# Where the low halves of the down weights come from: a subtraction on VectorE, or an accumulating transfer from GpSimd's queue

## The chip, the core and the metric

One core of a Trainium2 chip runs the whole program. The metric is device time in microseconds (us), the median of the runs taken. The engines are named as the profile names them: PE is TensorE (its matmuls), PEld its weight loads, DVE is VectorE, ACT is ScalarE, POOL is GpSimd, and SP the engine whose queue issues the loads.

## The reference

One layer over 256 tokens with a model width of 2048. What matters here are the two SwiGLU blocks, one near the start and one near the end, with 5632 hidden columns:

```python
def _swiglu(x, wg, wu, wd):
    return (jax.nn.silu(x @ wg) * (x @ wu)) @ wd

h = h + 0.5 * _swiglu(_rmsnorm(h, ffn1_norm[i]), ffn1_wg[i], ffn1_wu[i], ffn1_wd[i])
...
h = h + 0.5 * _swiglu(_rmsnorm(h, ffn2_norm[i]), ffn2_wg[i], ffn2_wu[i], ffn2_wd[i])
```

Between them stand an attention and short-convolution mixer with its own projections, and behind the second a gated embedding and a final norm. All weights are float32.

## The kernel before

Every weight matrix is streamed once from HBM in blocks of 512 rows by 512 columns. Such a block is a tile `raw` of 128 partitions by 2048 float32 values (1 MB); four `raw` buffers exist, and SP issues each load as soon as a buffer is free (`fetch`, line 84).

The products are made in three passes so as to keep float32 accuracy. Each operand is split into a high half `hi`, which is the value rounded to the float32r type that PE multiplies, and a low half `lo`, which is the rest. For every product `mm3` (line 100) issues three matmuls into the same PSUM bank: high by high (L101), high activations by low weights (L102), low activations by high weights (L103).

The weights are split on the way, half a `raw` tile (128 x 1024) at a time, by `split` (line 89): ACT copies the half into `whi`, which rounds it, and DVE subtracts `whi` from `raw` into `wlo`. There are five `whi` and five `wlo` buffers. One such half is here called a **step**; it feeds 12 matmuls: two blocks of 128 rows, two blocks of 128 tokens, three passes. Each step's first matmul (L101) waits for its `whi`, the next (L102) for its `wlo`.

`unit` (line 111) makes one output block of 512 columns: it loops over the `raw` tiles, over their two halves, and issues the matmuls. `pump` runs small queued pieces of work (transposes and splits of activations) between steps.

`swiglu` (line 230) goes through the 11 hidden blocks in three parts of 4, 4 and 3. In each part come the gate and up products of these blocks and the split of the gated result, and then the part's **down stage**: four `unit` calls with the name `ffn1d` or `ffn2d`, one for each 512 columns of the output, over the 4, 4 or 3 blocks just made. A down stage has 32, 32 or 24 steps, so there are 88 steps in each SwiGLU block and 176 in six stages overall. After each `unit` DVE adds half the result to `h` (line 266); in the third part the squares for the next norm follow on ACT.

The order within each engine is that of the program as written, with small moves by the scheduler; every engine works through its own queue in order, and a waiting instruction holds up what stands behind it.

Of the kernel before, what the change touches and what calls it, by code (L numbers as in the profile page):

```python
# [14 lines left out]
ALU = mybir.AluOpType  # L15
# [18 lines left out]
def block_kernel(ctx, tc, x, xT, pT, cols, fin, bias, mask,  # L34
                 wg1, wu1, wd1, win, wout, wg2, wu2, wd2, wpg, wpp, out):
    nc = tc.nc
# [6 lines left out]
    def act(out, in_, func=AF.Copy, **kw):  # L43
        nc.scalar.activation(out=out, in_=in_, func=func, **kw)  # L44
# [4 lines left out]
    def f(ap):  # L49
        return ap.bitcast(F32)  # L50
# [24 lines left out]
    def big(j, name):  # L75
        return (work.tile([P, 4, SEQ], F32R, tag=f"gh{j}", name=name + "h", bufs=1),
                work.tile([P, 4, SEQ], F32R, tag=f"gl{j}", name=name + "l", bufs=1))

    def wk(name):
        return work.tile([P, 512], F32, tag="wk", name=name, bufs=WK)  # L80
# [3 lines left out]
    def fetch(src, name):  # L84
        raw = wpool.tile([P, 2048], F32, tag="raw", name=f"raw_{name}", bufs=4)
        nc.sync.dma_start(out=raw, in_=src)
        return raw

    def split(raw, o, name, parts=1):
        hi = wpool.tile([P, 1024], F32R, tag="whi", name=f"whi_{name}", bufs=5)  # L90
        lo = wpool.tile([P, 1024], F32R, tag="wlo", name=f"wlo_{name}", bufs=5)
        n = 1024 // parts
        for i in range(parts):
            sl = slice(i * n, (i + 1) * n)
            rsl = slice(o + i * n, o + (i + 1) * n)
            act(hi[:, sl], raw[:, rsl])
            tt(out=lo[:, sl], in0=raw[:, rsl], in1=f(hi[:, sl]), op=ALU.subtract)  # L97
        return hi, lo

    def mm3(ps, xh, xl, wh, wl, first, last):  # L100
        nc.tensor.matmul(ps, lhsT=xh, rhs=wh, start=first, stop=False)  # L101
        nc.tensor.matmul(ps, lhsT=xh, rhs=wl, start=False, stop=False)  # L102
        nc.tensor.matmul(ps, lhsT=xl, rhs=wh, start=False, stop=last)  # L103
# [3 lines left out]
    def pump(n=1):  # L107
        for _ in range(min(n, len(queue))):
            queue.popleft()()

    def unit(w, n, name, lhs, flush_at=None, starting=False, hook=None):
        ps = [psum.tile([P, 512], F32, tag="mm", name=f"{name}_{t}") for t in range(2)]
        ng = 4 if flush_at is not None else len(lhs)
        for g in range(ng):
            if g == flush_at:
                pump(len(queue))
            if starting:
                raw = wpool.tile([P, 2048], F32, tag="raw", name=f"raw_{name}_{g}", bufs=4)
                m = 1 if g == 0 else 2
                for i in range(0, 4, m):  # L120
                    load_xT(g, i, m)
                    isl = slice(i * 512, (i + m) * 512)
                    nc.sync.dma_start(out=raw[:, isl], in_=w[n, g][:, isl])
            else:
                raw = fetch(w[n, g], f"{name}_{g}")
                if hook is not None:
                    hook(g)
            xh, xl = lhs[g]
            for s in range(2):
                hi, lo = split(raw, s * 1024, f"{name}_{g}_{s}", 2 if starting else 1)  # L130
                for j in range(2):
                    k = s * 2 + j
                    kk = g * 4 + k
                    for t in range(2):
                        tsl = slice(t * P, (t + 1) * P)
                        mm3(ps[t], xh[:, k, tsl], xl[:, k, tsl],
                            hi[:, j * 512:(j + 1) * 512], lo[:, j * 512:(j + 1) * 512],
                            kk == 0, kk == ng * 4 - 1)
                pump()
        return ps  # L140
# [20 lines left out]
    def rstd_of(which, only=None):  # L161
        nm = f"{which}_{only}"
        tsel = (0, 1) if only is None else (only,)
        n = len(tsel)
        s = small.tile([P, n], F32, tag="sm", name=f"sm_{nm}")
        for i, t in enumerate(tsel):
            nc.vector.tensor_reduce(out=s[:, i:i + 1], in_=stats[which, t][:, 0:nslot[which, t]],
                                    op=ALU.add, axis=AX.X)
        s2 = small.tile([P, n], F32, tag="sm2", name=f"sm2_{nm}")
        nc.vector.tensor_scalar(out=s2, in0=s, scalar1=1.0 / D, scalar2=EPS,  # L170
                                op0=ALU.mult, op1=ALU.add)
        r = small.tile([P, n], F32, tag="rstd", name=f"rstd_{nm}", bufs=4)
        nc.gpsimd.tensor_tensor(out=r, in0=s2, in1=mhalf[:, 0:n], op=ALU.pow)
        return r
# [15 lines left out]
    def finish_chunk(which, c):  # L190
        for p in range(2):
            queue.append(partial(next_aT, which, c, p))
        for t in range(2):
            square_stat(which, c, t)
# [3 lines left out]
    def load_xT(c, k0, n):  # L198
        if c not in xraw:
            xraw[c] = work.tile([P, 4, SEQ], F32, tag="y", name=f"xT_{c}", bufs=2)  # L200
        raw = xraw[c]
        nc.sync.dma_start(out=raw[:, k0:k0 + n, :],
                          in_=xT[c].rearrange("p (k s) -> p k s", k=4)[:, k0:k0 + n, :])
        for k in range(k0, k0 + n):
            g = col[:, c * 4 + k:c * 4 + k + 1]
            act(aTh[c][:, k, :], raw[:, k, :], scale=g)
            stt(out=aTl[c][:, k, :], in0=raw[:, k, :], scalar=g, in1=f(aTh[c][:, k, :]),
                op0=ALU.mult, op1=ALU.subtract)
# [21 lines left out]
    def swiglu(nm, nxt, wg, wu, wd, first):  # L230
        rstd = None
        chunk = 0
        for third, cnt in enumerate((4, 4, 3)):
            gs = []
            for j in range(cnt):
                fc = chunk + j
                pg = unit(wg, fc, f"{nm}g{fc}", aT, starting=first and fc == 0)
                if first and fc == 0:
                    pu = unit(wu, fc, f"{nm}u{fc}", aT, hook=load_x)
                if rstd is None:  # L240
                    rstd = rstd_of(nm)
                sg = []
                for t in range(2):
                    s = wk(f"{nm}sg{fc}_{t}")
                    act(s, pg[t], AF.Silu, scale=rstd[:, t:t + 1])
                    sg.append(s)
                if not (first and fc == 0):
                    pu = unit(wu, fc, f"{nm}u{fc}", aT)
                gt = []
                for t in range(2):  # L250
                    g = wk(f"{nm}gt{fc}_{t}")
                    stt(out=g, in0=pu[t], scalar=rstd[:, t:t + 1], in1=sg[t],
                        op0=ALU.mult, op1=ALU.mult)
                    gt.append(g)
                dst = big(j, f"{nm}g{fc}")
                for p in range(2):
                    queue.append(partial(pair_major, gt, p, f"{nm}gT{fc}", dst))
                gs.append(dst)
            last = third == 2
            wdt = wd[:, chunk:chunk + cnt]  # L260
            chunk += cnt
            for c in range(4):
                po = unit(wdt, c, f"{nm}d{third}_{c}", gs)
                for t in range(2):
                    hs = h[t][:, c * 512:(c + 1) * 512]
                    stt(out=hs, in0=po[t], scalar=0.5, in1=hs, op0=ALU.mult, op1=ALU.add)
                if last:
                    finish_chunk(nxt, c)

    swiglu("ffn1", "mix", wg1, wu1, wd1, True)  # L270

    rstd = rstd_of("mix")
# [181 lines left out]
    for c in range(4):  # L454
        po = unit(wout, c, f"o{c}", mixed, flush_at=3 if c == 0 else 4)
# [3 lines left out]
        finish_chunk("ffn2", c)  # L459

    swiglu("ffn2", "ple", wg2, wu2, wd2, False)

    rstd = rstd_of("ple")
# [24 lines left out]
    for c in range(4):  # L488
        if c % 2 == 0:
            raw = fetch(wpp[c // 2], f"pp{c}")  # L490
        hi, lo = split(raw, (c % 2) * 1024, f"pp{c}")
# [22 lines left out]
    for g in range(4):  # L514
        raw = fetch(wpg[3, g], f"pg3_{g}")
        xh, xl = aT[g]
        for s in range(2):
            hi, lo = split(raw, s * 1024, f"pg3_{g}_{s}")
# [110 lines left out]
```

## Time and profile before

| | us |
|---|---|
| median of 2 runs (1965.91 to 1966.38) | 1966.14 |
| span of the profiled execution | 1964.3 |
| PE busy in it | 1951.8 (99%) |
| DVE busy | 1039.3 (53%) |
| ACT busy | 902.6 (46%) |
| POOL busy | 35.2 (2%) |

The span runs from the first to the last instruction of the one profiled execution. It lies 1.8 us below the median of the runs, so a change worked out on the span is carried over to the median by adding 1.8 us.

### The profile page before, as it was taken

To read this page: it belongs to the slowest core of one execution; us is meant where nothing else is said; L and a number is where in the kernel's file an instruction comes from. 1 tells how busy PE (TensorE), PEld (TensorE's weight loads), DVE (VectorE), ACT (ScalarE), POOL (GpSimd) and SP (SyncE) were. 2 spreads that over 40 slices of the span, in tenths; PEclk is the share of its full clock that TensorE was granted. 3 is DMA by queue.
4 is the path that set the end of the run, shared out by engine and by line. 5 is a ranking of instruction groups with operands and counts; after the bars stand their busy time and mean duration, and the time that the engine had idled before them with its cause. 6 is when DMAs were issued, how large, how long until landed. Compare 5 with 4: busy or idle time off the path is not lost.

```text
span 1964.3 us, 21885 instructions
## 1 busy us (share of the span) xinstructions
PE 1951.8 (99%) x8889; PEld 1615.7 (82%) x8889; DVE 1039.3 (53%) x1064; ACT 902.6 (46%) x1121; POOL 35.2 (2%) x36
## 2 busy tenths in 40 slices
PE   9999999999999999999999999999999999999998
PEld 7888888888888888888888888888888888888886
DVE  5545554455545465665655554454445554445664
ACT  7444334444344454555545544443444433444554
POOL 0000000000000000110000000000000000000011
PEclk9999999999999999999999999999999999999999
DMA  9555555555555555544555555555555555555552
GB/s 353 199 190 192 193 193 193 190 186 187 194 193 187 193 179 185 193 172 161 182 184 186 180 190 193 190 186 195 195 185 188 190 193 193 193 192 184 201 182 105
DMA packets 55541, 374.01 MB, mean 190 GB/s; under 512 B 6416, under 2 KB 6928, under 8 KB 11408
## 3 DMA queue, kind: packets, MB, share of 16 engines
q1 hardware_dynamic: 55440, 372.62, 52.9%
q8 instruction: 69, 1.13, 0.2%
q14 instruction: 32, 0.26, 0.0%
HBM read 370.50 MB, written 2.10 MB: 190 GB/s over the span
## 4 chain that ended last, share of the span: by engine, by line
PE 99%; DMA 0%; issue 0%; SPq 0%; ACT 0%; DVE 0%; ACTq 0%; POOLq 0%; POOL 0%
PE ffn2g L101 4%; PE ffn2d L101 4%; PE ffn2g L103 4%; PE ffn1d L103 4%; PE ffn1d L101 4%; PE ffn2d L103 4%; PE ffn2g L102 4%; PE ffn2u L101 4%; PE ffn1u L101 4%; PE ffn1u L102 4%; PE ffn2d L102 4%; PE ffn2u L103 4%; PE ffn1u L103 4%; PE ffn2u L102 4%; PE ffn1d L102 4%; PE ffn1g L101 4%
## 5 line engine op out<-in xcount | busy, mean ns | idle before, releaser
L97 DVE TENSOR_TENSOR wlo_ffn2u<-raw_ffn2u,whi_ffn2u 128x1024 fp32r<-128x1024 f32 x88 | 107.8, 1226 | 131.6 <-ACT whi_ffn2u L44 131.6
L97 DVE TENSOR_TENSOR wlo_ffn1u<-raw_ffn1u,whi_ffn1u 128x1024 fp32r<-128x1024 f32 x88 | 107.5, 1226 | 124.0 <-ACT whi_ffn1u L44 124.0
L97 DVE TENSOR_TENSOR wlo_ffn2g<-raw_ffn2g,whi_ffn2g 128x1024 fp32r<-128x1024 f32 x88 | 107.9, 1226 | 112.9 <-ACT whi_ffn2g L44 112.9
L97 DVE TENSOR_TENSOR wlo_ffn1d<-raw_ffn1d,whi_ffn1d 128x1024 fp32r<-128x1024 f32 x88 | 107.9, 1226 | 112.2 <-ACT whi_ffn1d L44 112.2
L97 DVE TENSOR_TENSOR wlo_ffn2d<-raw_ffn2d,whi_ffn2d 128x1024 fp32r<-128x1024 f32 x88 | 107.9, 1226 | 111.4 <-ACT whi_ffn2d L44 111.4
L97 DVE TENSOR_TENSOR wlo_ffn1g<-raw_ffn1g,whi_ffn1g 128x1024 fp32r<-128x1024 f32 (+1 forms) x96 | 108.2, 1136 | 101.7 <-ACT whi_ffn1g L44 101.7
L44 ACT ACTIVATE whi_ffn2g<-raw_ffn2g 128x1024 fp32r<-128x1024 f32 x88 | 93.4, 1061 | 141.2 <-PE ffn2u L103 66.4
L44 ACT ACTIVATE whi_ffn1g<-raw_ffn1g 128x1024 fp32r<-128x1024 f32 (+1 forms) x96 | 94.2, 988 | 133.7 <-PE ffn1u L103 63.0
L44 ACT ACTIVATE whi_ffn1d<-raw_ffn1d 128x1024 fp32r<-128x1024 f32 x88 | 93.4, 1061 | 135.2 <-PE ffn1d L103 110.3
L44 ACT ACTIVATE whi_ffn2d<-raw_ffn2d 128x1024 fp32r<-128x1024 f32 x88 | 93.4, 1061 | 133.8 <-PE ffn2d L103 108.9
L44 ACT ACTIVATE whi_ffn2u<-raw_ffn2u 128x1024 fp32r<-128x1024 f32 x88 | 93.2, 1060 | 120.3 <-PE ffn2g L103 73.1
L44 ACT ACTIVATE whi_ffn1u<-raw_ffn1u 128x1024 fp32r<-128x1024 f32 x88 | 92.8, 1059 | 113.6 <-PE ffn1g L103 66.4
L101 PE MATMUL ffn1g<-whi_ffn1g,aTh 128*128 128x512 f32 x352 | 138.1, 395 | 1.5 <-ACT whi_ffn1g L44 1.5
L101 PE MATMUL ffn2g<-whi_ffn2g,aTh 128*128 128x512 f32 x352 | 138.8, 394 | 0.0
L102 PE MATMUL ffn1g<-wlo_ffn1g,aTh 128*128 128x512 f32 x352 | 137.3, 390 | 0.0
L103 PE MATMUL ffn1g<-whi_ffn1g,aTl 128*128 128x512 f32 x352 | 137.2, 390 | 0.0
L103 PE MATMUL ffn2g<-whi_ffn2g,aTl 128*128 128x512 f32 x352 | 137.2, 390 | 0.0
L102 PE MATMUL ffn2g<-wlo_ffn2g,aTh 128*128 128x512 f32 x352 | 137.0, 389 | 0.0
L101 PE MATMUL ffn1u<-whi_ffn1u,aTh 128*128 128x512 f32 x352 | 136.9, 389 | 0.0
L102 PE MATMUL ffn1u<-wlo_ffn1u,aTh 128*128 128x512 f32 x352 | 136.9, 389 | 0.0
L103 PE MATMUL ffn1u<-whi_ffn1u,aTl 128*128 128x512 f32 x352 | 136.9, 389 | 0.0
L101 PE MATMUL ffn2u<-whi_ffn2u,aTh 128*128 128x512 f32 x352 | 136.9, 389 | 0.0
(442 smaller groups left out, 4433.3 us busy)
## 6 DMA issues: line engine op xcount, KB each, us to landing
raw_ffn1u<-in_wu SPq DMA_DIRECT2D x44, 1024.0 KB, 4.8
raw_ffn1d<-in_wd SPq DMA_DIRECT2D x44, 1024.0 KB, 4.8
raw_ffn2g<-in_wg SPq DMA_DIRECT2D x44, 1024.0 KB, 4.8
raw_ffn2u<-in_wu SPq DMA_DIRECT2D x44, 1024.0 KB, 4.8
raw_ffn2d<-in_wd SPq DMA_DIRECT2D x44, 1024.0 KB, 4.8
raw_ffn1g<-in_wg SPq DMA_DIRECT2D x40, 1024.0 KB, 4.8
raw_o<-in_wout SPq DMA_DIRECT2D x16, 1024.0 KB, 4.8
raw_pg<-in_wpg SPq DMA_DIRECT2D x16, 1024.0 KB, 4.8
```

The source lines that it names most:

```text
L44: nc.scalar.activation(out=out, in_=in_, func=func, **kw)
L97: tt(out=lo[:, sl], in0=raw[:, rsl], in1=f(hi[:, sl]), op=ALU.subtract)
L101: nc.tensor.matmul(ps, lhsT=xh, rhs=wh, start=first, stop=False)
L102: nc.tensor.matmul(ps, lhsT=xh, rhs=wl, start=False, stop=False)
L103: nc.tensor.matmul(ps, lhsT=xl, rhs=wh, start=False, stop=last)
```

## The change

In the down stages, and only there (`acc=True`), the low half is made in another way. ACT writes the rounded weights into `whi` as before and in a second pass the negated rounded weights into `wlo`. Then a transfer issued from GpSimd's queue reads the same half block of raw weights from HBM a second time and adds it onto `wlo` in place. DVE takes no part. The `raw` tile is still loaded, since ACT reads it.

```diff
-    def split(raw, o, name, parts=1):
+    def split(raw, o, name, parts=1, src=None):
         hi = wpool.tile([P, 1024], F32R, tag="whi", name=f"whi_{name}", bufs=5)
         lo = wpool.tile([P, 1024], F32R, tag="wlo", name=f"wlo_{name}", bufs=5)
+        if src is not None:
+            act(hi, raw[:, o:o + 1024])
+            act(lo, raw[:, o:o + 1024], scale=-1.0)
+            nc.gpsimd.dma_start(out=lo, in_=src[:, o:o + 1024], accum_op=ALU.add)
+            return hi, lo
...
-                hi, lo = split(raw, s * 1024, f"{name}_{g}_{s}", 2 if starting else 1)
+                hi, lo = split(raw, s * 1024, f"{name}_{g}_{s}", 2 if starting else 1,
+                               src=w[n, g] if acc else None)
...
-                po = unit(wdt, c, f"{nm}d{third}_{c}", gs)
+                po = unit(wdt, c, f"{nm}d{third}_{c}", gs, acc=True)
```

On ACT, at the start of the first down stage (`ffn1d_0_0_0` is part 0's first column block, first `raw` tile, first half), this stands in the queue before:

```order
L44 ACTIVATE whi_ffn1u_3_1_1363<-raw_ffn1u_3_1345 128x1024 [waits DVE_49,PE_49]
L44 ACTIVATE whi_ffn1d_0_0_0_1389<-raw_ffn1d_0_0_1387 128x1024 [waits DMAHW6_49,DVE_49,PE_49]
L44 ACTIVATE whi_ffn1d_0_0_1_1412<-raw_ffn1d_0_0_1387 128x1024 [waits DVE_49,PE_49]
L44 ACTIVATE whi_ffn1d_0_1_0_1437<-raw_ffn1d_0_1_1435 128x1024 [waits DMAHW7_49,DVE_49,PE_49]
L44 ACTIVATE whi_ffn1d_0_1_1_1453<-raw_ffn1d_0_1_1435 128x1024 [waits DVE_49,PE_49]
```

and this now:

```order
L44 ACTIVATE whi_ffn1u_3_1_1363<-raw_ffn1u_3_1345 128x1024 [waits DVE_49,PE_49]
L44 ACTIVATE wlo_ffn1d_0_0_0_1390<-raw_ffn1d_0_0_1387 128x1024 [waits DMAHW6_49,DVE_49,PE_49]
L44 ACTIVATE whi_ffn1d_0_0_0_1389<-raw_ffn1d_0_0_1387 128x1024 [waits PE_49,Activation_49]
L44 ACTIVATE wlo_ffn1d_0_0_1_1414<-raw_ffn1d_0_0_1387 128x1024 [waits DVE_49,PE_49]
L44 ACTIVATE whi_ffn1d_0_0_1_1413<-raw_ffn1d_0_0_1387 128x1024 [waits PE_49,Activation_49]
L44 ACTIVATE wlo_ffn1d_0_1_0_1440<-raw_ffn1d_0_1_1437 128x1024 [waits DMAHW7_49,DVE_49,PE_49]
```

ACT has two copies a step where it had one, the negated one first; each waits for PE to be through with the buffer that it overwrites.

On POOL the same place was empty: between the preparations for the attention and the next norm stood nothing.

```order
L173 TENSOR_TENSOR rstd_ffn_None<-sm_ffn_None,mhalf 128x2 [waits DVE_49,Pool_49]
L349 TENSOR_TENSOR bm_0_0_5513<-bm_0_0_5513,msk 128x512 [waits DMAHW4_49,DMAHW3_49]
L349 TENSOR_TENSOR bm_0_1_5550<-bm_0_1_5550,msk 128x512 [waits DMAHW6_49]
L173 TENSOR_TENSOR rstd_mix_None<-sm_mix_None,mhalf 128x2 [waits DVE_49]
L349 TENSOR_TENSOR bm_1_0_5589<-bm_1_0_5589,msk 128x512 [waits DMAHW1_49,DVE_49]
```

Now the 88 transfers of the first SwiGLU block stand there in a row, each of them behind its ACT copy:

```order
L355 TENSOR_TENSOR bm_0_0_5601<-bm_0_0_5601,msk 128x512 [waits DMAHW4_49,DMAHW3_49]
L355 TENSOR_TENSOR bm_0_1_5638<-bm_0_1_5638,msk 128x512 [waits DMAHW6_49]
L95 DMA wlo_ffn1d_0_0_0_1390<-in_wd 128x1024 [waits Activation_49]
L95 DMA wlo_ffn1d_0_0_1_1414<-in_wd 128x1024 [waits Activation_49]
L95 DMA wlo_ffn1d_0_1_0_1440<-in_wd 128x1024 [waits Activation_49]
```

Only the work on the attention bias `bm`, long done by then, and the norms stand beside them on that queue.

On PE the order is the same as before; what changes is whom a step's second matmul waits for. Before:

```order
L103 MATMUL ffn1u_1_1242<-whi_ffn1u_3_1_1363,aTl_103 128x512
L101 MATMUL ffn1d_0_0_1385<-whi_ffn1d_0_0_0_1389,ffn1g0h 128x512 [waits Activation_49]
L102 MATMUL ffn1d_0_0_1385<-wlo_ffn1d_0_0_0_1390,ffn1g0h 128x512 [waits DVE_49]
L103 MATMUL ffn1d_0_0_1385<-whi_ffn1d_0_0_0_1389,ffn1g0l 128x512
L101 MATMUL ffn1d_0_1_1386<-whi_ffn1d_0_0_0_1389,ffn1g0h 128x512
```

and now (the lines are numbered five higher in the changed file):

```order
L108 MATMUL ffn1u_1_1242<-whi_ffn1u_3_1_1363,aTl_103 128x512
L106 MATMUL ffn1d_0_0_1385<-whi_ffn1d_0_0_0_1389,ffn1g0h 128x512 [waits Activation_49]
L107 MATMUL ffn1d_0_0_1385<-wlo_ffn1d_0_0_0_1390,ffn1g0h 128x512 [waits DMASW0_49]
L108 MATMUL ffn1d_0_0_1385<-whi_ffn1d_0_0_0_1389,ffn1g0l 128x512
L106 MATMUL ffn1d_0_1_1386<-whi_ffn1d_0_0_0_1389,ffn1g0h 128x512
```

The wait for DVE has become a wait for a transfer from GpSimd's queue.

## Rows read from the trace of the kernel before

**Rows 1.** The page: busy time, share of the span and instructions of each engine.

```profile
PE 1951.8 (99%) x8889; PEld 1615.7 (82%) x8889; DVE 1039.3 (53%) x1064; ACT 902.6 (46%) x1121; POOL 35.2 (2%) x36
```

**Rows 2.** The page: the chain that ended last, by engine.

```profile
PE 99%; DMA 0%; issue 0%; SPq 0%; ACT 0%; DVE 0%; ACTq 0%; POOLq 0%; POOL 0%
```

**Rows 3.** The six down stages: length, busy us of each engine, PE clock, DMA share, GB/s.

```profile
core 0: us, PE busy (x) PEld busy (x) DVE busy (x) ACT busy (x) POOL busy (x), PEclk, DMA share, GB/s
185.20:272.90 87.70, 87.70 (x392) 72.62 (x391) 45.06 (x42) 34.92 (x34) 0.00 (x0) 1.00 0.54 192
449.90:538.10 88.20, 88.20 (x394) 73.03 (x393) 45.56 (x44) 34.92 (x34) 0.00 (x0) 1.00 0.54 191
670.30:738.90 68.60, 68.60 (x320) 56.76 (x319) 40.33 (x47) 35.28 (x50) 0.00 (x0) 1.00 0.51 184
1300.10:1388.20 88.10, 88.10 (x394) 72.92 (x394) 45.46 (x44) 34.92 (x34) 0.00 (x0) 1.00 0.54 191
1565.60:1653.00 87.40, 87.40 (x391) 72.38 (x390) 44.76 (x42) 34.83 (x34) 0.00 (x0) 1.00 0.54 193
1785.00:1854.00 69.00, 69.00 (x322) 57.08 (x321) 41.42 (x48) 35.92 (x51) 0.00 (x0) 1.00 0.53 190
sum 489.00, PE 489.00 PEld 404.79 DVE 262.60 ACT 210.80 POOL 0.00; mean PE 81.50 PEld 67.47 DVE 43.77 ACT 35.13 POOL 0.00
```

**Rows 4.** The tile raw_ffn1d: ns min/median/max, first and last start, form; then landing times.

```profile
L44 ACT ACTIVATE whi_ffn1d<-raw_ffn1d x88: 1059/1061/1064, 174.5 to 725.3; 128x1024 fp32r<-128x1024 f32 x88
L97 DVE TENSOR_TENSOR wlo_ffn1d<-raw_ffn1d,whi_ffn1d x88: 1225/1226/1227, 175.6 to 726.4; 128x1024 fp32r<-128x1024 f32 x88
L86 SPq DMA_DIRECT2D raw_ffn1d<-in_wd x44: 327/328/328, 157.8 to 705.0; - x44
...
  PE ffn1d L103: 110.3, 69
...
DMA to landing us min/median/max: 4.6/4.8/5.4
```

**Rows 5.** The first 50 us, when the loads run unchecked; columns as in rows 3.

```profile
10.00:20.00 10.00, 9.28 (x37) 6.43 (x37) 8.20 (x17) 8.91 (x19) 0.00 (x0) 1.00 0.99 350
20.00:30.00 10.00, 10.00 (x45) 8.28 (x45) 7.02 (x11) 5.95 (x11) 0.00 (x0) 1.00 1.02 417
30.00:40.00 10.00, 10.00 (x45) 8.26 (x44) 4.92 (x6) 9.26 (x21) 0.00 (x0) 1.00 1.01 423
```

**Rows 6.** The page: DMA queues with packets, MB and share of 16 engines.

```profile
q1 hardware_dynamic: 55440, 372.62, 52.9%
q8 instruction: 69, 1.13, 0.2%
q14 instruction: 32, 0.26, 0.0%
HBM read 370.50 MB, written 2.10 MB: 190 GB/s over the span
```

**Rows 7.** ACT and PE around 185 us: the fifth step's copy, and matmuls that use it (first start 197.0).

```profile
185.41 1.06 ACT L44 ACTIVATE whi_ffn1d<-raw_ffn1d 128x1024 fp32r<-128x1024 f32 x1 [1.66 <-PE ffn1u L103]
L101 PE MATMUL ffn1d<-whi_ffn1d,ffn1g2h x32: 389/389/389, 197.0 to 267.1; 128*128 128x512 f32 x32
```

**Rows 8.** DMA issues: count, KB each, median us from issue to landing; small loads among them.

```profile
raw_ffn1g<-in_wg SPq DMA_DIRECT2D x6, 512.0 KB, 7.0
h<-in_x SPq DMA_DIRECT2D x2, 1024.0 KB, 14.7
xT<-in_xT SPq DMA_DIRECT2D x6, 256.0 KB, 5.9
```

More of the change, by code (lines that the diff above doesn't have):

```diff
@@ L109, in pump, with unit @@
             queue.popleft()()
-    def unit(w, n, name, lhs, flush_at=None, starting=False, hook=None):
+    def unit(w, n, name, lhs, flush_at=None, starting=False, hook=None, acc=False):
         ps = [psum.tile([P, 512], F32, tag="mm", name=f"{name}_{t}") for t in range(2)]
```

## The prediction

> **What bounds the kernel now.** I read the busy times first, then the chain that ended last, and then cut out the six down stages, since only they change. PE is busy 1951.8 of 1964.3 us [rows 1] and makes 99% of the chain [rows 2]. Inside the down stages there is no gap at all: 489.0 us, all of them PE [rows 3]. That settles two things. First, taking work off DVE can give nothing by itself: DVE waits for ACT and PE waits for neither. All that PE is not busy in the whole span is 1964.3 - 1951.8 = 12.5 us, or 0.6%, so no cure of waits can make the kernel 2% faster. Second, the question is only whether the new source of `wlo` keeps up with PE, which uses one half block every 489.0 / 176 = 2.78 us.
>
> What feeds a stage is read from the same rows: DMA engines busy 0.51 to 0.54 of the time for 184 to 193 GB/s, ACT 34.9 of 87.7 us, DVE 45.1 of 87.7 us. At full stretch the DMA engines moved 417 and 423 GB/s with a share of 1.01 to 1.02, in a stretch of 1 MB loads, and 350 GB/s at a share of 0.99 ten microseconds earlier, when loads of 256 and 512 KB were among them [rows 5, 8]. That is their ceiling here.
>
> **The change part by part.**
>
> *The subtraction on DVE goes.* 176 x 1.226 us = 216 us of DVE time [rows 4], worth nothing to the end, since PE never waited for it.
>
> *A second copy on ACT comes.* 176 x 1.061 us = 187 us [rows 4]; the negated copy reads and writes the same form as the one that the row shows. In a stage of 32 steps ACT goes from 34.9 to 68.9 of 87.7 us; in the third part, with its squares, from 35.3 + 24 x 1.061 to 60.7 of 68.6 us [rows 3], 88%. ACT stays under PE's pace, and the copies are done ahead of use, so I cost this at nothing. The cover is thin in the third part: were ACT to need more than 2.78 us a step there, it would be late next. Each copy waits for PE to leave the old buffer, as the present one does for 69 of 88 copies [rows 4]; behind it on ACT stand the next step's copies and the splits of activations, which have the same slack as today.
>
> *GpSimd's queue gets 176 issues.* Its own work is 35.2 us in the whole span [rows 1] and none in a down stage [rows 3], and what stands behind a waiting transfer there is the next transfer. SP's issue of a load of twice the size takes 0.328 us [rows 4]; the trace has no issue from GpSimd's queue [rows 6]. Anything up to 2.78 us per issue is hidden, and I cost it at nothing; beyond that it is part of the second rival.
>
> *The latency of the new chain.* Before, the fifth step's copy starts on ACT at 185.41 us and the matmuls that use it start at 197.0 us [rows 7]: a lead of 11.6 us. Of that the negated copy takes 1.06 us and an issue about 0.33 us, which leaves some 10.2 us for the transfer. A plain load of 1 MB lands 4.8 us after its issue in a stage that is half busy [rows 4], one of 512 KB in the crowded start after 7.0 us [rows 8]. Both fit. Latency alone costs nothing, as long as several transfers are in flight.
>
> *The bytes.* This is the term that decides. Per step a stage moves half of a `raw` tile, 0.524 MB. The new transfer reads the same 0.524 MB from HBM again, and to add it onto `wlo` it also has to fetch the 0.524 MB that ACT has put there: two operands read for one result written. If each operand costs the DMA engines what a loaded byte costs, a step moves 3 x 0.524 = 1.573 MB in place of 0.524. The trace shows no such transfer, so I bound it. Lower end: the second operand is free, and the step is 1.049 MB per 2.78 us = 377 GB/s, which is under 420: hidden, cost 0. Middle, both operands counted: the plain load at 420 GB/s takes 1.25 us; the 1.049 MB of the accumulation take 2.50 us at 420 GB/s and 3.00 us at the 350 GB/s of the stretch with smaller transfers [rows 5]. The new transfers are of 512 KB, between the two kinds, so I take 385 GB/s, 2.72 us. The step is then 1.25 + 2.72 = 3.97 us (3.75 to 4.25), which is 1.19 us (0.97 to 1.47) over PE's pace. Upper end: the transfers go one after another, each with its whole time to landing; that is a rival below.
>
> I take the middle because the DMA engines' rows show them saturated by bytes moved, and the second operand must come through something.
>
> The Trainium skill, in "Collectives: The Full Stack", section "The bandwidth ceiling: the fold count and why AG ≠ RS ≠ AR", says that a DMA that adds runs at half the rate of one that copies, because it reads two sources through one ring. No row here shows it; by it the accumulation would be 2.5 us at the ceiling of the rows, the low end of the middle case.
>
> *How many steps pay.* Five `wlo` buffers can be filled while the up product before the stage still runs. In those 5 x 2.78 = 13.9 us the DMA engines have 0.46 x 13.9 = 6.4 us to spare [rows 3], good for 6.4 / 2.72 = 2.3 accumulations. Over six stages 14 of 176 steps are paid from idle time, and 162 are not.
>
> *Sum.* 162 x 1.19 = 193 us (157 to 238) on a span of 1964.3 us: 2157, and with the 1.8 us between span and median **2159 us** (2123 to 2204). PE then stands still some 1.2 us in each step, at L107. The rows show the granted clock at 1.00, the 2.4 GHz level, in every stretch read, also where PE was busy 9.28 of 10 us [rows 5]; no row has PE standing still in every step. At the lower level of 1.2 GHz a step's matmuls would take 5.56 us, and the sum would be 162 x 2.78 = 450 us, 2416; I count that as a way into the range, not as the forecast.
>
> **The rivals.**
>
> *Hidden after all (not slower).* The operand that lies in SBUF costs the DMA engines nothing beside the one that comes from HBM. Then a step needs 377 GB/s of a ceiling of about 420, landing at 4.8 to 7.0 us is inside the 10.2 us of lead, and the end does not move: 1966 us. For it: there is room, 0.54 twice is 1.08 by share, but by bytes only 90%. Against it: that 1.08, and 90% leaves no room for anything that a smaller transfer costs more. It decides at a step of 2.78 us, which is 1.3 us or so for the whole accumulation.
>
> The Trainium skill, in "DMA: Bandwidth & Descriptors", section "Anatomy of one DMA — SWDGE (gpsimd) path", gives a transfer from GpSimd's queue about 2.0 us plus its bytes by 436 GB/s. As an estimate from that page 512 KB would land after 3.2 us and this rival would hold; it speaks of copies, and no row here shows it.
>
> *Far slower: the accumulations don't overlap.* GpSimd's queue, or the read, add and write of each piece, works off one transfer before the next makes progress. Then a step takes a whole time to landing. With 4.8 us [rows 4] it is (4.8 - 2.78) x 162 = 327 us, 2293 us; with the 7.0 us of the crowded 512 KB loads [rows 8] 4.22 x 162 = 684 us, 2650 us. It also covers an issue on GpSimd that itself takes longer than 4 us. For it: nothing of this kind is in the trace, and it is a read, a sum and a write per piece. Against it: plain loads overlap well, five buffers are in play, and several queue entries wait only for ACT.
>
> *Doing something else.* Were the transfers reordered far from their steps the waits would fall elsewhere; the order on GpSimd's queue shows them in the order of use, so I give that no chance of its own.
>
> **How the numbers follow.** A measurement of this kernel tells about 2% (39 us) from no change. Bytes decide, with its own range of 2123 to 2204: 0.50. Far slower: 0.35, of which I put 0.10 above 2650. Hidden: 0.14. Faster by over 2%: 0.01, for the 12.5 us bound above. The chance of within 2% is that of the hidden case, 0.14, and slower has 0.85. For the range I leave out the hidden case and the end above 2650 (0.24 together), but pull the low end down to 1995 to hold a step that comes out only just over PE's pace, which brings what is left out to about 0.2.
>
> **What the profile afterwards would show.** DMA share near 1.0 in the six stages and a stage of 32 steps at some 120 us where it took 88 [rows 3]; PE idle before the matmuls on `wlo` (L107), released by the transfer; HBM reads up from 370.5 by 176 x 0.524 = 92 MB [rows 6]; DVE down by 216 us and ACT up by 187 us; the gate and up stages unchanged. If PE's idle time ends on ACT, the ACT term was wrong; if the DMA share is well under 1 while PE waits, it is the second rival; if PE has no gaps, the second operand was free. The forecast is wrong first of all if my price for an accumulated byte is: it stands on no row of its own.

## The result, and the profile after

The changed kernel takes 2138.26 us (median of 2 runs, 2137.66 to 2138.87) against 1966.14 us before; the ratio is 1.0876, with a 95% interval of 1.0844 to 1.0907. The profiled execution spans 2137.1 us, 172.8 us more than before.

The page of the changed kernel, its busy times, then its DMA queues (packets, MB, share of 16 engines' span), then the chain that ended last:

```profile
PE 2002.0 (94%) x8889; PEld 1610.2 (75%) x8889; DVE 829.7 (39%) x888; ACT 1067.3 (50%) x1297; POOL 187.5 (9%) x212
...
q1 hardware_dynamic: 55440, 372.62, 47.3%
q0 software_dynamic: 25344, 92.29, 21.9%
...
HBM read 462.77 MB, written 2.10 MB: 218 GB/s over the span
...
PE 45%; issue 31%; DMA 21%; ACT 1%; POOL 1%; DVE 0%; POOLq 0%; SPq 0%; ACTq 0%
```

Beside [rows 1, 2, 6]: DVE has lost 209.6 us, ACT gained 164.7 us, a second DMA queue (q0) carries 92.29 MB, and the chain that was PE alone now runs through transfers. (The 31% of "issue" in that chain are no loss of their own: the page of experiment 1 below has 32% there, and PE is not held up.) PE's busy time rose by 50.2 us for the same 8889 matmuls, so the loss of 172.8 us shows as 122.6 us more of idle time and these 50.2 us. At least in part this is how a pause is drawn: a matmul that follows a wait counts 0.50 us (rows further below) where it counts 0.39 us in an unbroken row [rows 7]. The share of the queue gives the price of one transfer: 0.219 x 2137.1 us / 176 = 2.66 us of all 16 DMA engines for 0.524 MB landed.

The three down stages of the first SwiGLU block, columns as in rows 3:

```profile
185.10:306.80 121.70, 97.11 (x395) 71.12 (x394) 12.29 (x16) 61.54 (x63) 24.15 (x28) 1.00 1.01 273
483.30:603.60 120.30, 96.97 (x395) 70.98 (x394) 12.18 (x16) 61.43 (x63) 24.19 (x28) 1.00 1.03 277
735.70:822.00 86.30, 72.08 (x309) 53.75 (x308) 15.87 (x25) 52.40 (x69) 17.25 (x20) 1.00 1.05 284
```

The first stage took 87.70 us and takes 121.70, the second 88.20 and 120.30 [rows 3]. PE is busy 97 of 121.7 us, ACT 61.5, and the one thing that is full is the DMA share, 1.01 to 1.05 where it was 0.51 to 0.54. (The third row's window ends about 4 us before that stage's last step.) The share is the sum of the packets' times over 16 engines; as it goes over 1, packets must overlap a little, and it is not exact to some per cent. The GB/s beside it, 273 to 284, look as if there were room below the 420 of the start [rows 5]; they count what lands (92.29 MB are 176 times 0.524 MB), so a second operand, if one is fetched, is not in them.

The tile wlo_ffn1d: GpSimd's issue (ns min/median/max), who waited for the tile (us, times), landing times:

```profile
L95 POOL DMA_DIRECT2D wlo_ffn1d<-in_wd x88: 853/862/1048, 175.6 to 810.0; - x88
...
  PEld ffn1d L107: 95.0, 79
  PE ffn1d L107: 62.8, 75
...
DMA to landing us min/median/max: 6.8/14.7/17.4
```

PE's wait is at L107, for the transfer, as forecast: 79 of 88 steps. The 95.0 us of the weight load and the 62.8 us of the matmul are the same pause seen by two parts of PE, and are not added. The landing of 14.7 us invites another reading, that latency is the bound; the experiments take that up.

A steady piece of the first stage (40 us), its queues and their issues:

```profile
q0 software_dynamic: 1551, 5.64, 70.9%
q1 hardware_dynamic: 764, 5.47, 34.0%
...
wlo_ffn1d<-in_wd POOLq DMA_DIRECT2D x11, 512.0 KB, 14.8
```

With 144 packets to a transfer (25344 / 176) these are 10.8 transfers in 28.4 us, 2.63 us each, and 5.47 MB of loads in 13.6 us, 1.30 us for each half block. Together they are 3.93 us a step, at a total share of 1.05, so 3.75 us by the clock: the pace of the step.

### The profile page after: what moved, and what is told of

It reads as the page before. It is cut to its first block, busy times and chain, and to the rows that moved or that the text cites. A ratio compares the mean times of both kernels' runs of the same rounds, so it can differ in the third digit from the quotient of the medians.

```text
span 2137.1 us, 22367 instructions
## 1 busy us (share of the span) xinstructions
PE 2002.0 (94%) x8889; PEld 1610.2 (75%) x8889; DVE 829.7 (39%) x888; ACT 1067.3 (50%) x1297; POOL 187.5 (9%) x212
## 3 DMA queue, kind: packets, MB, share of 16 engines
q0 software_dynamic: 25344, 92.29, 21.9%
## 4 chain that ended last, share of the span: by engine, by line
PE 45%; issue 31%; DMA 21%; ACT 1%; POOL 1%; DVE 0%; POOLq 0%; SPq 0%; ACTq 0%
DMA wlo_ffn1d<-in_wd 10%; DMA wlo_ffn2d<-in_wd 10%; PE ffn1g L106 2%; PE ffn1g L108 2%; PE ffn1g L107 2%; PE ffn1u L106 2%; PE ffn1u L107 2%; PE ffn1u L108 2%; PE ffn2g L106 1%; PE ffn2g L108 1%; PE ffn2g L107 1%; PE ffn2u L106 1%; PE ffn2u L107 1%; PE ffn2u L108 1%; PE pg L108 1%
## 5 line engine op out<-in xcount | busy, mean ns | idle before, releaser
L44 ACT ACTIVATE wlo_ffn1d<-raw_ffn1d 128x1024 fp32r<-128x1024 f32 x88 | 93.1, 1058 | 130.7 <-PE ffn1d L107 117.9
L44 ACT ACTIVATE wlo_ffn2d<-raw_ffn2d 128x1024 fp32r<-128x1024 f32 x88 | 93.1, 1057 | 124.3 <-PE ffn2d L107 111.4
L95 POOL DMA_DIRECT2D wlo_ffn2d<-in_wd x88 | 76.0, 864 | 723.3 <-ACT wlo_ffn2d L44 709.1
L107 PE MATMUL ffn1g<-wlo_ffn1g,aTh 128*128 128x512 f32 x352 | 137.6, 391 | 0.0
L107 PE MATMUL ffn2g<-wlo_ffn2g,aTh 128*128 128x512 f32 x352 | 137.0, 389 | 0.0
L107 PE MATMUL ffn1u<-wlo_ffn1u,aTh 128*128 128x512 f32 x352 | 136.9, 389 | 0.0
L107 PE MATMUL ffn2u<-wlo_ffn2u,aTh 128*128 128x512 f32 x352 | 136.9, 389 | 0.0
## 6 DMA issues: line engine op xcount, KB each, us to landing
wlo_ffn1d<-in_wd POOLq DMA_DIRECT2D x88, 512.0 KB, 14.7
```

Source lines behind the costliest of these rows:

```text
L95: nc.gpsimd.dma_start(out=lo, in_=src[:, o:o + 1024], accum_op=ALU.add)
```

## The experiments

**The theory**: the accumulation has to fetch two operands, the added one (the source) and the one that lies in `wlo` (the destination); the 16 DMA engines pay for both, and they are full; a step takes what they need. **The rivals**: a transfer from GpSimd's queue is slow as such (issue, conversion); the second read of HBM is the bound; the chain of copy, issue, landing and use is too long for five buffers; ACT's second copy is late; a piece is read, added and written in turn, at a cost by the piece; the adder is slow by the element.

All of them start from the changed kernel. Ratios are against the kernel before.

**1. A copy in place of the addition.**

```diff
-            nc.gpsimd.dma_start(out=lo, in_=src[:, o:o + 1024], accum_op=ALU.add)
+            nc.gpsimd.dma_start(out=lo, in_=src[:, o:o + 1024])
```

> The transfer from GpSimd's queue copies the raw half block onto the low half instead of adding it; everything else, ACT's two copies and the order of the waits included, is as in the changed kernel. The low half is then the whole weight, so the product is another one than the reference's. Theory (two operands are paid): the copy has one operand and costs the DMA engines about 0.524 MB at 400 GB/s = 1.3 us in place of the 2.64 us measured, a step needs 2.6 us of them against PE's 2.78, and the time goes back to 1966 to 1985 us, with GpSimd's DMA queue at about 11 or 12% of the engines' span. Rival (what is slow is a transfer from GpSimd's queue as such, by its issue or its conversion to float32r, not the addition): 2.64 us stay and the time is 2120 to 2145 us.

Measured: 1970.57 us, ratio 1.0021 (1.0012 to 1.0030). The page's queue, and the stage that lay at 185 to 273 us before:

```profile
q0 software_dynamic: 25344, 92.29, 13.8%
```

```profile
185.10:272.90 87.80, 87.80 (x393) 72.72 (x392) 11.30 (x14) 61.46 (x62) 14.77 (x28) 1.00 1.01 371
```

The same bytes land through the same queue in the same number of packets, and PE has no gap. A copy costs 0.138 x 1968.1 / 176 = 1.54 us where the addition costs 2.66. So the queue as such, the second read of HBM (371 GB/s now pass in the stage) and ACT's part are not the cause. The 1.54 us are more than the 1.3 expected, and the DMA share is at 1.01: a copy seems only just to fit. The issue on GpSimd is shorter for a copy (0.527 us for 0.862), so this run alone does not clear it; experiment 5 does.

**2. The raw weights from SBUF, not from HBM.**

```diff
-            nc.gpsimd.dma_start(out=lo, in_=src[:, o:o + 1024], accum_op=ALU.add)
+            nc.gpsimd.dma_start(out=lo, in_=raw[:, o:o + 1024], accum_op=ALU.add)
```

> The transfer adds the raw half block from the tile that already lies in SBUF, not from HBM; the result is the same. Theory (the DMA engines' own time for two operands is the bound, wherever they lie): 2.64 us per transfer and 2125 to 2150 us, with HBM reads back at 370 MB. Rival (the second read of HBM is the bound): without it a step is back to the load that the kernel before had, 1966 to 1990 us. Beside these, tiles of raw weights are held until the transfer has read them, which can only add a little.

Measured: 2131.42 us, ratio 1.0839 (1.0821 to 1.0857). The page's queue and HBM lines:

```profile
q0 software_dynamic: 25344, 92.29, 22.0%
...
HBM read 370.50 MB, written 2.10 MB: 175 GB/s over the span
```

HBM is read as little as before the change, and the time hardly moves: 0.220 x 2135.2 / 176 = 2.67 us a transfer. Where the added operand lies hardly matters: from SBUF the kernel is 7 us faster, of the 172 us lost.

**3. Six buffers for the low halves.**

```diff
-        lo = wpool.tile([P, 1024], F32R, tag="wlo", name=f"wlo_{name}", bufs=5)
+        lo = wpool.tile([P, 1024], F32R, tag="wlo", name=f"wlo_{name}", bufs=6)
```

> Six buffers for the low halves in place of five, nothing else. Theory (DMA engines saturated): the step stays at 3.75 us, landing grows by about one step to some 18 us, and the time is 2120 to 2140 us. Rival (the chain of copy, issue, landing at 14.7 us and use, about 19.5 us, is the bound and is shared among the buffers): the step falls from 19.5 / 5 = 3.9 to 19.5 / 6 = 3.25 us and the time by about 0.6 x 176 = 105 us, to 2030 to 2060 us.

Measured: 2136.60 us, ratio 1.0868 (1.0852 to 1.0884). Landing times of wlo_ffn1d:

```profile
DMA to landing us min/median/max: 8.6/18.5/21.4
```

One more transfer in flight makes each land 3.8 us later, one step, and the pace stays. The 14.7 us were a queue in front of full engines, not a latency that set the pace.

**4. ACT's part alone**, VectorE adding the raw weights:

```diff
-            nc.gpsimd.dma_start(out=lo, in_=src[:, o:o + 1024], accum_op=ALU.add)
+            tt(out=lo, in0=raw[:, o:o + 1024], in1=f(lo), op=ALU.add)
```

> ACT's part of the change alone: it writes the high half and the negated high half as in the changed kernel, and VectorE, not a transfer, adds the raw weights onto the latter. Theory (only the transfers cost): ACT stays under PE's pace at 88% or less, and the time is that of the kernel before, 1962 to 1975 us. Rival (the second copy on ACT, with its waits for PE, is part of the loss): 2000 us or more.

Measured: 1966.70 us, ratio 1.0001 (0.9992 to 1.0011). The page's busy times:

```profile
PE 1951.8 (99%) x8889; PEld 1617.1 (82%) x8889; DVE 1041.1 (53%) x1064; ACT 1067.8 (54%) x1297; POOL 36.7 (2%) x36
```

ACT's second copy is hidden, as the prediction had it, and so is the fact that each `wlo` passes through two engines.

**5. One load of raw weights a stage.**

```diff
+    kept = {}
...
-                raw = fetch(w[n, g], f"{name}_{g}")
+                if acc and not (n == 0 and g == 0):
+                    raw = kept["raw"]
+                else:
+                    raw = fetch(w[n, g], f"{name}_{g}")
+                    kept["raw"] = raw
```

> In a down stage the raw tile is loaded only once and ACT makes every high and negated half from that one tile; the transfers from GpSimd's queue go on as in the changed kernel. This leaves out 43 of 44 loads (or 31 of 32, 23 of 24 by stage: all but the first of each stage), so the weights multiplied are other ones. It measures the accumulations without company. Theory (two bills on one set of engines add up: 2.64 us for the accumulation and 1.3 us for the load): 2.64 us alone are just under PE's 2.78, and the time is 1966 to 1990 us, with the DMA share in the down stages at 0.93 to 1.0. Rival (an accumulation is limited by its own chain, not by what it shares): the step stays near 3.75 us and the time above 2100 us.

(The transfers add the block's own weights, so both halves together are still the block; it is the high half that is another block's, and with it the product with the low activations. A stage has 16, 16 or 12 loads, one for two steps, so the edit leaves out 41 of 44 loads in each SwiGLU block, not 43: three `raw_ffn1d` loads are left.)

Measured: 1971.35 us, ratio 1.0024 (1.0015 to 1.0034). The stage from 190 to 270 us, then the tile's landing times:

```profile
190.00:270.00 80.00, 80.00 (x357) 66.21 (x356) 8.33 (x11) 56.14 (x57) 22.49 (x26) 1.00 1.03 200
```

```profile
DMA to landing us min/median/max: 5.5/7.2/9.9
```

Without the loads beside them the accumulations keep PE's pace and land in half the time, and GpSimd issues them as slowly as in the changed kernel (0.865 us each). So the loads and the accumulations share one thing and their costs add up, and GpSimd's issue is not what held PE up. The DMA share was expected at 0.93 to 1.0 and is 1.03. By it an accumulation takes 0.254 x 1966.8 / 176 = 2.84 us, over PE's 2.78, and still PE has no gap: a share just over 1 is not yet a loss, and a price read from it can be some per cent too high. Accumulations alone come close to filling the engines; that they fill them is not shown.

**6. Every other half block.**

```diff
-                               src=w[n, g] if acc else None)
+                               src=w[n, g] if acc and s == 1 else None)
```

> Only the second half of each raw tile gets its low half by the accumulating transfer, the first by VectorE as before; the result is the same. Theory (bytes of the DMA engines): two steps need 2 x 1.3 + 2.64 = 5.2 us of them against 5.56 us of PE, so all is hidden: 1966 to 1985 us, DMA share in the down stages 0.9 to 0.97. Rival (waits from each transfer, by its latency, or a cost that every issue has on the path): half the loss stays, about 2050 us.

Measured: 1978.74 us, ratio 1.0063 (1.0047 to 1.0080). The stage from 190 to 270 us, then the queues from 220 to 260 us:

```profile
190.00:270.00 80.00, 77.61 (x341) 62.97 (x340) 22.12 (x23) 42.90 (x43) 11.31 (x14) 1.00 1.00 275
...
q0 software_dynamic: 1011, 3.69, 52.7%
q1 hardware_dynamic: 999, 7.27, 47.0%
```

Half the transfers cost 12.2 us, not half of the 172 us. That is the behaviour of a ceiling: nothing up to it, everything beyond. The share is 1.00, over the 0.9 to 0.97 expected, and PE has small gaps; the demand was above my sum of 5.2 us. In the 40 us of the second piece 7.02 accumulations (1011 / 144) took 21.1 us, 3.00 us each, and 13.9 half blocks of loads 18.8 us, 1.36 us each: two steps need 2 x 1.36 + 3.00 = 5.72 us where PE needs 5.56.

**7. Each accumulation in two transfers.**

```diff
-            nc.gpsimd.dma_start(out=lo, in_=src[:, o:o + 1024], accum_op=ALU.add)
+            for i in range(2):
+                nc.gpsimd.dma_start(out=lo[:, i * 512:(i + 1) * 512],
+                                    in_=src[:, o + i * 512:o + (i + 1) * 512], accum_op=ALU.add)
```

> Each accumulation is issued as two transfers of 128 x 512, so that its pieces are of 2 KB and twice as many, for the same bytes. Theory (the cost goes by operand bytes): 2130 to 2190 us. Rival (the cost goes by the piece, some 0.33 us for each of an engine's eight, for a read, an addition and a write in turn): an accumulation takes 5.3 us, the step about 6.5 us, and the time is above 2500 us.

Measured: 2153.27 us, ratio 1.0949 (1.0933 to 1.0965). The page's queue:

```profile
q0 software_dynamic: 50688, 92.30, 23.7%
```

Twice the packets for the same bytes cost 0.237 x 2152.6 / 176 = 2.90 us in place of 2.66. So a piece has a price of at most about (2.90 - 2.66) / 8 = 0.03 us for each of the eight that an engine has more (an estimate), far from the 0.33 us of the rival. The time rose by less, 15 us or 0.09 us a step, and the granted clock was below 1.00 in this run's stages (0.94 over 500 to 560 us), so not all of that need be the pieces.

**8 and 9. Operand bytes or elements.** The theory still had two readings: two operands to fetch, or an adder that takes so long for each element. A constant tile as source, in bf16 and in float32, keeps the elements and changes the bytes of one operand:

```diff
+    half = cpool.tile([P, 1024], BF16, name="half")
+    nc.gpsimd.memset(half, 0.0)
...
-            nc.gpsimd.dma_start(out=lo, in_=src[:, o:o + 1024], accum_op=ALU.add)
+            nc.gpsimd.dma_start(out=lo, in_=half, accum_op=ALU.add)
```

> The accumulation reads a constant tile of zeros in bf16 from SBUF instead of the raw weights, with the same number of elements; the destination stays as it is. The low half is then the negated high half, so the product is another one than the reference's. It asks what the 2.65 us of an accumulation are. Theory (operand bytes): 2 + 4 bytes an element in place of 4 + 4, three quarters of the bytes, about 2.0 us a transfer, step about 3.1 us, and 2010 to 2050 us. Rival (the speed of the addition, by the element): 2.6 us or more stay, and the time is that of the float32 source beside it, about 2130 us.

> The twin of the run with a bf16 source: the constant tile of zeros is float32, all else the same; the low half is again the negated high half. Both theories expect the time of the run with the raw tile in SBUF as source, 2120 to 2140 us, and 2.6 to 2.7 us a transfer; if reading one and the same tile over and over costs anything of its own it shows here.

Measured: bf16 2034.30 us, ratio 1.0343 (1.0325 to 1.0360); float32 2154.20 us, ratio 1.0961 (1.0940 to 1.0983). The queue on the page of the bf16 run:

```profile
q0 software_dynamic: 25344, 92.29, 17.8%
```

and of the float32 run:

```profile
q0 software_dynamic: 25344, 92.29, 22.1%
```

That is 0.178 x 2033.1 / 176 = 2.06 us against 0.221 x 2151.7 / 176 = 2.70 us: three quarters of the operand bytes, 76% of the time, at the same number of elements and packets. An adder that takes its time by the element alone is refuted: the source is paid by its bytes, 0.64 us for the 2 bytes an element that it has less. The times agree: the bf16 run is 120 us faster than its twin, 0.68 us a step. That the rest, about 1.1 us more than a copy, is the fetch of the destination and not an addition beside it is not shown: no run changes the destination. It is inferred from the size, since 4 bytes of source at this rate are 1.28 us. The price is read from the queue here and not from the total, since the bf16 run's DMA share in its first stage is 0.97 and PE still waits in places. The float32 twin is 14 us over its expected range and 23 us over the run with the raw tile as source, with nearly the same share per transfer; why is not settled.

## Why the prediction was right, point by point

It was right in direction, mechanism and, nearly, in size: 2159 us forecast, with 2123 to 2204 for the case, and 2138 measured.

- *PE is the bound before, and DVE's work is worth nothing.* Confirmed: experiments 1 and 5 take the subtraction off DVE and are not faster than the kernel before (ratios 1.0021 and 1.0024).
- *ACT's second copy at nothing.* Confirmed by experiment 4. ACT's busy time rose by 165 us rather than 187, since two copies in a row overlap: in the trace the second starts 0.97 us after the first, which lasts 1.06.
- *GpSimd's issue at nothing.* Right in effect, by experiment 5; an issue takes 0.862 us, not about 0.33.
- *Latency at nothing.* Right, though the landing of 14.7 us is over the lead of 10.2 us that I had worked out. The order is the other way round: the queue before full engines makes the landing long. Experiment 3 shows it, and experiment 5 shows 7.2 us where the loads are gone.
- *The bytes.* This is the term that decided, as forecast. The price was 2.72 us for an accumulation and 1.25 for the load; measured are 2.63 to 2.66 and 1.30. Their sum, 3.97 us in the forecast and 3.93 measured, was taken as the step; the step is 3.75 us, since the packets of the two queues overlap a little (share 1.05). This is the term that was too large: 0.97 us over PE's pace in place of 1.19. That the price of the accumulation came out so close is partly luck: I priced its two operands alike, at 1.36 us each, from loads of another queue; measured, a copy through GpSimd's queue takes 1.54 us and the addition 1.1 us more.
- *Steps paid from idle time.* The second term that was mis-sized: I let 162 of 176 steps pay, and nothing was saved in the total. The weight loads waited in 79 + 76 = 155 steps (the second block's row has 76), but the loss over all 176 is 172.8 / 176 = 0.98 us, what the pace of 3.75 us gives if every step pays. The transfers did start 10 us ahead of the first stage, at 175.56 us, and yet this stage lost 34.0 us and the second 32.1. What the start gave, the end seems to have taken back; no run separates the two. PE's waits at the end of the first stage:

```profile
300.27 0.50 PE L107 MATMUL ffn1d<-wlo_ffn1d,ffn1g3h 128*128 128x512 f32 x1 [0.40 <-DMA wlo_ffn1d<-in_wd]
303.71 0.50 PE L107 MATMUL ffn1d<-wlo_ffn1d,ffn1g3h 128*128 128x512 f32 x1 [0.42 <-DMA wlo_ffn1d<-in_wd]
```

The last transfer, issued at 289.28 us, is waited for until 303.71 us, and PE's last step comes after it, while the DMA share has fallen to 0.43 (300 to 306 us). With all 176 steps paying, 176 x 0.97 = 171 us, against 172.8 us measured. So the two sizes that were off, 1.19 for 0.97 and 162 for 176, went in opposite directions and left 20 us of the 193.
- *The clock.* The way to 2416 us was not taken, but the clock did not stay at 1.00 throughout. It did in the three stages of the first SwiGLU block; in those of the second, and in ten microseconds of the last one, with the ten before them, the rows are:

```profile
1386.50:1506.80 120.30, 97.14 (x394) 72.00 (x393) 11.92 (x15) 61.38 (x62) 24.16 (x28) 0.99 1.02 275
1683.70:1803.70 120.00, 98.25 (x393) 71.81 (x392) 11.82 (x15) 61.36 (x62) 24.16 (x28) 0.99 1.02 276
1936.20:2027.30 91.10, 76.10 (x321) 57.22 (x320) 18.25 (x28) 53.64 (x71) 17.25 (x20) 0.98 1.04 286
...
1960.00:1970.00 10.00, 7.35 (x36) 5.64 (x35) 1.93 (x4) 5.88 (x10) 1.72 (x2) 1.00 1.04 313
1970.00:1980.00 10.00, 7.99 (x28) 5.92 (x27) 0.00 (x0) 4.56 (x5) 1.72 (x2) 0.83 1.05 277
```

So each of these stages was in small part at 1.2 GHz, after PE had stood still in steps (7.35 us busy in the ten before the last fall). By the rows the three lack about 4 us of full clock (an estimate: 1% of 120 us twice and 2% of 91), and they are not longer than the stages of the first block: this is no large part of the 172.8 us.
- *The rival that nothing changes.* It asked for a free second operand; experiment 1 shows that the addition costs about 1.1 us over a copy, and experiment 2 that this does not depend on where the source lies. The threshold of "1.3 us or so" that I gave it does not follow from my own numbers: 2.78 - 1.25 leaves 1.53 us for the transfer, and the copy, at 1.54 us, was hidden.
- *The rival of transfers that don't overlap.* Refuted by experiment 5: the same transfers through the same queue keep PE's 2.78 us a step once the loads are gone. (Experiment 3 alone would not do, since a queue that works off one transfer at a time would not gain by a sixth buffer either.)

The rule of the Trainium skill that I set beside the term, in "Collectives: The Full Stack", section "The bandwidth ceiling: the fold count and why AG ≠ RS ≠ AR", says of a collective, ReduceScatter, that adding halves the rate through the second read, not through the addition. The runs here agree in that the source is paid by its bytes; they do not separate the read of the destination from the addition, and the ratio measured is 2.66 / 1.54 = 1.7, not 2.

## What to carry to other kernels

A transfer that adds cost the engines 1.7 times one that copies here, close to a bill for both operands, and the GB/s of the profile count only what lands: work out the engines' load as operand bytes, and read the DMA share, not the GB/s. Then look at PE as well, since a share of 1.01 or 1.03 stood beside an unbroken PE in experiments 1 and 5. Moving work from an engine with time to spare to the DMA engines pays nothing while PE is the bound, and costs everything beyond the point at which loads and additions together fill them; half of the transfers cost 12 us here, all of them 172. A long landing time beside a share of 1.0 was a queue here, and another buffer only lengthened it.

## What the runs showed of the hardware that was not expected

- The price of a transfer of 128 x 1024 from GpSimd's queue lies near a line, if the destination of an addition is counted as an operand: 1.54 us for 4 operand bytes an element, 2.06 for 6, 2.66 to 2.70 for 8. That is about 1.1 us for each 0.524 MB fetched and about 0.4 us beside. In experiments 5 and 6 the same accumulation took 2.84 and 2.94 us, so the price also depends on what runs beside it; how is not settled.
- GpSimd's issue of an accumulation took 0.862 us, that of a copy of the same shape 0.527 us:

```profile
L95 POOL DMA_DIRECT2D wlo_ffn1d<-in_wd x88: 527/527/747, 175.7 to 729.2; - x88
```

- In runs in which PE waited in most steps the granted clock fell for short times. In the float32 twin it was 0.97 on the mean over 185.10 to 300.00 us, so in part at the lower of its two levels (1.2 and 2.4 GHz), with PE busy 92.22 of 114.90 us; in experiment 2 it was 0.93 over 750 to 800 us, with PE busy 41.84 of 50:

```profile
185.10:300.00 114.90, 92.22 (x371) 68.85 (x369) 9.03 (x12) 59.61 (x61) 24.06 (x28) 0.97 1.05 276
...
750.00:800.00 50.00, 41.84 (x171) 31.83 (x170) 7.42 (x14) 32.35 (x45) 11.18 (x13) 0.93 1.05 274
```

PE waits for transfers there anyway. The clock does not explain why the twin is 23 us slower than experiment 2: the mean granted clock of the four runs of each is 0.985 to 0.992 in the twin and 0.985 to 0.990 in experiment 2.
